# A scan's rows stored, summed and normed one chunk later in the transfers' order

## The chip, the cores and the metric

The kernel runs on one core of a Trainium2 chip. The metric is the device time of one execution in microseconds; the kernel before took a median of 1601.38 us over three runs (1596.47 to 1603.47). The engines are TensorE (PE, with its weight loads PEld), VectorE (DVE), ScalarE (ACT), GpSimd (POOL) and SyncE (SP). SP computes nothing here: it issues most of the transfers, strictly one after the other.

## The reference

The input is one sequence of 1024 tokens with 1024 features. Two layers follow each other, each `h = h + W_out(mixer(rmsnorm(h)) * silu(z))`, and a last RMSNorm. Layer 0 is a chunked spatial gate. Layer 1 is a Mamba-2 mixer, and the change lies in it:

```python
cb = jnp.einsum('bclgn,bcsgn->bclsg', Cm, Bm)
w_ls = (cb[..., None] * decay * dt[:, :, None])
y_diag = jnp.einsum('bclsgj,bcsgjp->bclgjp', w_ls, x)
states = jnp.einsum('bclgn,bclgj,bclgjp->bcgjpn', Bm, decay_to_end * dt, x)
_, prev = lax.scan(step, init, (states, chunk_decay))
y_off = jnp.einsum('bclgn,bcgjpn,bclgj->bclgjp', Cm, prev, jnp.exp(dA_cs))
y = y_diag + y_off + x * d_skip
gated = rmsnorm((y * silu(z)) per group of 256, norm_w)
return gated @ w_out
```

There are 8 groups of 256 inner features (4 heads of 64) and 8 chunks of 128 tokens. Within a group the chunks hang on each other by the carried state. The gated rows of each group are normed over the group's 256 features, token by token, and then multiplied by the output weights.

## The kernel before, in words

Layer 1's scan is one loop over 56 chunks, groups 0 to 6 with 8 chunks each (`scans`, L1705). Group 7 comes after it (`last_steps`, L1677), woven into the first products with the output weights. The scan stands in a region whose order is written by hand: every engine, SP's queue too, issues the region's instructions in the order in which the code names them. What follows the region is ordered by a planner, by estimated times, and may be put between them.

One step of the loop, for chunk `n`, names in this order: the chunk's products on PE (`pe_b`, L1576: `yy` from the decay-weighted matrix and the carried state, L1582 and L1586, and the new state's sum `sp`, L1593); some matmuls of the projection that makes a later group's `x`, `B` and `C` (`project`, tiles `ab`, with weight loads `wr` and splits at L111 and L112); the transposes for chunk n+2 (`pe_a`, `tp`); the state's update and the chunk's output on VectorE (L1612, L1618, L1621); the weights of chunk n+1 (L1573); the decay of chunk n+2 on ScalarE (L1555, L1557); the carried state on GpSimd (L1603); the tokens of chunk n+2 (L1563 to L1568); the gate, which multiplies the output into the `z` rows on GpSimd (L1628); one queued step of the convolution for the projected group (L1281, L1287); and the load of the decay rows of chunk n+3 (`load`, L1544, tile `wl`, four buffers).

Rows come and go by half groups of four chunks. `prefetch` (L1505) loads for a half group `xbc` (only in groups 0, 1, 3 and 5, whose projections were made earlier and spilt), and `ze`: two rows of `z` (L1513) and four broadcast rows of decays (`ecs`, L1517). It is named at chunk 0 for the second half of the same group, and at chunk 4 for the first half of the next. In groups 2, 4, 6 and 7 `x` and `bc` come straight from the projection, which starts a new `x` or `bc` tile at chunk 4 of each group.

A finished half group is treated in the next half. At chunk 4 or 0 its gated rows, which lie in its `ze` tile, are squared on ScalarE (L1633, tile `gsq`) and stored (L1635, to `g_d`). At chunk 5 or 1 GpSimd adds the two rows of squares (L1638). At chunk 7 or 3 PE sums them over the features within `pe_b` (L1645), ScalarE copies the sums to a small tile `srow` (L1649), and SP stores them (`sum_c`, L1652, to `ss_d`). `group_rstd` (L1655) reads the sums of a whole group back as a column (`sv`, L1660) at chunk 4 of the next group; VectorE and GpSimd work out the reciprocal root at chunk 6 (L1666, L141) and chunk 7 (L150 to L153, tile `rvv`), and SP stores it (L1673, to `rs_d`). The output products read `g_d` and `rs_d` later (L1813, L1805).

Tiles of one tag share a fixed number of buffers. A new tile waits until all that used its buffer are done, transfers included:

```python
def s8(shape, name, dt=F32):
    return sb.tile(shape, dt, name=name, tag="s8", bufs=16)
def q4(shape, name):
    return sb.tile(shape, F32, name=name, tag="q4", bufs=6)
```

`s8` buffers (8 KB per partition) hold the split input of the projections (`hh` and `hl` for four quarters, 8 tiles), the table of token values `tk`, and every `x`, `bc`, `xbc` and `ze`. `q4` buffers hold `cw`, the working tile of a chunk, and `gsq`. `k2` holds `wl`; `k1` (three buffers) holds the carried state, a product `t1`, and `srow`.

Of the kernel before, what the change touches and what calls it, by code (L numbers as in the profile page):

```python
# [8 lines left out]
F32 = mybir.dt.float32  # L9
# [6 lines left out]
P = 128  # L16
# [6 lines left out]
G = 8  # L23
# [6 lines left out]
def kernel(  # L30
# [21 lines left out]
    nc = tc.nc  # L52
    x = x[0]
    out = out[0]
# [22 lines left out]
    def tiny(shape, name):  # L77
        return sb.tile(shape, F32, name=name, tag="tiny", bufs=8)
# [65 lines left out]
    def rsqrt_b(dst, v, r, n, rows=P):  # L144

        u = tiny([P, 8], "ru")[:rows, :n]
        if n == 1:
            nc.vector.scalar_tensor_tensor(u, r, v, r, ALU.mult, ALU.mult)
        else:
            nc.vector.tensor_tensor(u, r, r, ALU.mult)  # L150
            nc.vector.tensor_tensor(u, u, v, ALU.mult)
        nc.vector.tensor_scalar(u, u, -0.5, 1.5, ALU.mult, ALU.add)
        nc.vector.tensor_tensor(dst, r, u, ALU.mult)  # L153
# [398 lines left out]
    for gp in range(G // 2):  # L552
# [4 lines left out]
        if gp == 1:  # L557
# [9 lines left out]
            for h in range(2):  # L567
# [9 lines left out]
                for k in range(4):  # L577
                    g = h * 4 + k
# [941 lines left out]
    class Scan:  # L1520
# [110 lines left out]
        def squares(self, th):  # L1631
            sq = self.sq = q4([P, 2, 512], "gsq")
            nc.scalar.activation(sq, self.z(4 * th, 4), AF.Square)  # L1633
            if self.g < G - 1:
                nc.sync.dma_start(out=gd[self.g][:, :, th * 512:(th + 1) * 512], in_=self.z(4 * th, 4))  # L1635

# [3 lines left out]
        def sum_b(self, pr=None):  # L1640
            pr = sm("pr") if pr is None else pr
            n = 1 if self.g < G - 1 else 2
            for m in range(n):
                for h in range(2):
                    nc.tensor.matmul(out=pr[h * 64:h * 64 + 1, 0:256], lhsT=ones[:, 0:1],  # L1645
                                     rhs=self.sq[:, m, h * 256:(h + 1) * 256], start=m == 0, stop=m == n - 1)
            self.sr = sb.tile([P, 256], F32, name="srow", tag="k1", bufs=3)
            for h in range(2):
                nc.scalar.copy(out=self.sr[h * 64:h * 64 + 1], in_=pr[h * 64:h * 64 + 1, 0:256])  # L1649

# [4 lines left out]
    def group_rstd(g, t0, n):  # L1655


        c = n // P
        sv = tiny([P, 8], "sv")[:, 0:c]
        nc.sync.dma_start(out=sv, in_=ss_d[g, t0:t0 + n].rearrange("(p c) -> p c", c=c))  # L1660
        behind = lambda i: nullcontext() if i is None else tc.issue_after(i.ins)
        got = []

        def guess(after=None):
            with behind(after):
                nc.vector.tensor_scalar(sv, sv, 1.0 / 256, NORM_EPS, ALU.mult, ALU.add)  # L1666
                got.append(rsqrt_a(sv, c))

        def tail(after=None, queue=nc.gpsimd):
            rv = tiny([P, 8], "rvv")[:, 0:c]  # L1670
            with behind(after):
                rsqrt_b(rv, sv, got[0], c)
            queue.dma_start(out=rs_d[g, t0:t0 + n].rearrange("(p c) -> p c", c=c), in_=rv)  # L1673

        return guess, tail

    def last_steps():  # L1677

        sc = Scan(G - 1, V)

        def a(c):
            sc.load(c), sc.pe_a(c), sc.decay(c), sc.tokens(c), sc.weights(c)

        a(0)
        yield
        for c in range(8):
            if c < 7:
                a(c + 1)
                yield
            sc.pe_b(c), sc.carry(c), sc.update(c), sc.out(c)  # L1690
            last = sc.gate(c)
            if c == 1:
                prefetch(G - 1, 1)
                rs = group_rstd(G - 2, 0, T)
            if c in (2, 3):
                rs[c - 2](last)
            if c % 4 == 3:
                sc.squares(c // 4), sc.sum_b(), sc.sum_c(c // 4)
            if c == 3:
                half = group_rstd(G - 1, 0, 512)  # L1700
            if c in (4, 5):
                half[c - 4](last)
            yield

    def scans():  # L1705

        chunks = [(g, c) for g in range(G - 1) for c in range(8)]
        N = len(chunks)
        scan, rs, ran = {}, {}, [0]
        total = 32 * len(plain)  # L1710

        def project(upto):
            while ran[0] < upto:
                next(pj, None)
                ran[0] += 1

        def at(f, n, *a):
            if 0 <= n < N:
                g, c = chunks[n]
                if g not in scan:  # L1720
                    scan[g] = Scan(g, nc.gpsimd)
                getattr(scan[g], f)(c, *a)

        prefetch(0, 0)
        project(AHEAD // 2 + 1)
        while todo or late:
            convolve()
        for n in range(2):
            at("load", n)
        drain(1)  # L1730
        for n in range(2):
            at("decay", n)
        drain(len(queue))
        at("pe_a", 0), at("tokens", 0), at("weights", 0)
        drain(len(queue))
        project(AHEAD)
        at("pe_a", 1), at("tokens", 1), at("weights", 1)
        at("load", 2)
        for n, (g, c) in enumerate(chunks):
            want = lambda f: AHEAD + (total - AHEAD) * (n + f) // N  # L1740
            p = g if c >= 4 else g - 1
            at("pe_b", n, scan[p] if c % 4 == 3 and p >= 0 else None)
            project(want(.5))
            at("pe_a", n + 2)
            at("update", n)
            at("out", n)
            if n > 0:
                at("weights", n + 1)
            at("decay", n + 2)
            at("carry", n + 1)  # L1750
            at("tokens", n + 2)
            at("gate", n)
            drain()
            at("load", n + 3)
            th = 0 if c >= 4 else 1
            if p >= 0:
                sc = scan[p]
                if c % 4 == 0:
                    sc.squares(th)
                elif c % 4 == 1:  # L1760
                    sc.sum_a()
                elif c % 4 == 3:
                    sc.sum_c(th)
            if g > 0:
                if c == 4:
                    rs[g] = group_rstd(g - 1, 0, T)
                elif c == 6:
                    rs[g][0]()
                elif c == 7:
                    rs[g][1](None, nc.sync)  # L1770
            if c == 0:
                prefetch(g, 1)
            if c == 4:
                prefetch(g + 1, 0)
            project(want(1))
        project(total)
        sc = scan[G - 2]
        drain(len(queue))
        sc.squares(1), sc.sum_a(), sc.sum_b(), sc.sum_c(1)

    def interleave(a, na, b, nb):

# [80 lines left out]
    def into_end():  # L1863
        rs7 = []

        def hook(n, c):
            if (n, c) == (2, 0):
                bo.fetch(2, 2)
                rs7.extend(group_rstd(G - 1, 512, 512))
                rs7[0]()  # L1870
                bo.fetch(22, 0)
            elif (n, c) == (2, 1):
                bo.fetch(2, 3)
                rs7[1](None, nc.scalar)
                bo.fetch(22, 1)
                bo.sums(2, 0)
            elif (n, c) == (2, 2):
                bo.fetch(22, 2)
                bo.sums(2, 1)
            elif (n, c) == (2, 3):  # L1880
                bo.fetch(22, 3)
                bo.sums(2, 2)
            elif n in (6, 4):
                if (n, c) == (6, 0):
                    bo.sums(2, 3)
                if c % 2:
                    bo.fetch({6: 4, 4: 5}[n], c - 1)
                bo.sums(n, c)
                if (n, c) == (6, 2):
                    weigh_left(0)  # L1890
            elif n == 5:
                bo.prep_last(c)
                if c == 1:
                    weigh_left(1)
                if c == 3:
                    bo.prep_unit(0)

        bo.ran = Out.ORDER
        for n in (2, 6, 4, 5):
            for _ in bo.product(n, hook):  # L1900
                pass
        bo.prep_unit(1)
        r1 = bo.rstd_half(1)
        for tt in range(4):
            bo.last_mm(tt)
            if 0 < tt < 3:
                bo.prep_unit(tt + 1)
            if tt:
                bo.post(3, tt - 1)
                bo.rstd_a(0, tt - 1)  # L1910
            finish_b(1, tt, r1[:, tt:tt + 1])
            if tt:
                finish_b(0, tt - 1, bo.rstd_b(0, tt - 1))
        bo.post(3, 3)
        bo.rstd_a(0, 3)
        finish_b(0, 3, bo.rstd_b(0, 3))
# [33 lines left out]
```

## Time and profile before

| | |
|---|---|
| median of three runs | 1601.38 us (1596.47 to 1603.47) |
| the profiled execution's own time | 1599.88 us |
| its span, first to last instruction | 1598.2 us |
| TensorE busy, share of the span | 1506.0 us, 94% |
| VectorE, ScalarE, GpSimd busy | 1055.3, 777.0, 418.7 us |
| mean granted TensorE clock | 0.973 |
| scan of groups 0 to 6, from the first chunk | 1069 to 1360 us |

Each row of a timeline gives the start in us, the duration in us, the engine, the source line, the operation and the tiles, written ahead of read ones, and in brackets the idle time before it and what ended it. Rows of one line that follow each other are merged with their count. `SPq` is SP's queue: a gap between two of its rows is time in which the next transfer waited for a buffer, for its data, or for an earlier transfer. A wait is put down to what ended last.

### The profile page before, as it was taken

The numbers are of one execution on the slowest core, as the hardware profiler recorded it, in microseconds if no ns is written. First come the engines' busy times: TensorE is split into PE (matmuls) and PEld (weight loads), VectorE is DVE, ScalarE is ACT, GpSimd is POOL, SyncE is SP. The second block draws the span as 40 slices with busy tenths as digits, with TensorE's granted clock in tenths as the row PEclk, the third lists the DMA queues.
The fourth block names the chain that finished last, engine by engine and source line by source line (L and its number), as shares of the span: only waits on it lengthen the run. The fifth ranks groups of instructions, "written<-read, shape, count | busy, mean of one in ns | idle before, by whom it ended". The sixth has DMA issues, their size and how long they took to land.

```text
span 1598.2 us, 21253 instructions
## 1 busy us (share of the span) xinstructions
PE 1506.0 (94%) x7834; PEld 1239.8 (78%) x7834; DVE 1055.3 (66%) x1706; ACT 777.0 (49%) x1247; POOL 418.7 (26%) x443
## 2 busy tenths in 40 slices
PE   5799999999999999998999999989999999979988
PEld 4799988888888887876788787767777777757766
DVE  7966566666666554777637377757777767658656
ACT  4522233323222354555555455646766677544444
POOL 3601010000000131220011312126777765231231
PEclk7999999999999999999999999999999999989999
DMA  5153332332333999755367878776565665795992
GB/s 173 41 191 127 105 109 100 110 111 97 111 108 125 323 261 256 162 139 129 105 154 177 165 165 158 174 208 194 156 176 160 194 172 145 238 249 174 229 237 107
DMA packets 176919, 260.21 MB, mean 163 GB/s; under 512 B 16320, under 2 KB 102960, under 8 KB 173616
## 3 DMA queue, kind: packets, MB, share of 16 engines
q1 hardware_dynamic: 124992, 169.45, 34.3%
q0 software_dynamic: 41888, 71.58, 23.0%
q10 hardware_dynamic: 9936, 17.83, 3.1%
q8 instruction: 62, 1.02, 0.3%
q14 instruction: 41, 0.34, 0.1%
HBM read 185.61 MB, written 51.18 MB: 148 GB/s over the span
## 4 chain that ended last, share of the span: by engine, by line
PE 59%; issue 14%; DMA 9%; DVE 9%; ACT 6%; POOL 1%; ACTq 0%; SPq 0%; POOLq 0%; DVEq 0%
PE acc L136 10%; PE acc L134 9%; PE acc L135 9%; PE ab L134 4%; PE ab L136 4%; PE ab L135 4%; DMA ya<-ya 2%; PE yy L1582 2%; DMA wl<-cs_d 2%; PE yy L1586 2%; PE ao L134 2%; PE ao L135 2%; PE ao L136 2%; PE sp L1593 2%; ACT wh L111 2%
## 5 line engine op out<-in xcount | busy, mean ns | idle before, releaser
L134 PE MATMUL acc<-hh,wh 128*128 128x512 f32 x868 | 343.9, 396 | 15.4 <-ACT u L292 7.6
L136 PE MATMUL acc<-hh,wl 128*128 128x512 f32 x868 | 341.6, 394 | 1.7 <-DVE wl L112 1.6
L135 PE MATMUL acc<-hl,wh 128*128 128x512 f32 x868 | 340.8, 393 | 0.0
L134 PEld LDWEIGHTS acc<-hh,wh 128*128 128x128 f32 x868 | 164.8, 190 | 52.3 <-ACT u L292 9.3
L112 DVE TENSOR_TENSOR wl<-wr,wh 128x1024 fp32r<-128x1024 f32 (+1 forms) x99 | 118.1, 1194 | 128.2 <-ACT wh L111 128.1
L136 PEld LDWEIGHTS acc<-hh,wl 128*128 128x128 f32 x868 | 164.5, 190 | 40.2 <-DVE wl L112 5.6
L135 PEld LDWEIGHTS acc<-hl,wh 128*128 128x128 f32 x868 | 164.8, 190 | 33.4
L111 ACT CAST wh<-wr 128x1024 fp32r<-128x1024 f32 (+1 forms) x113 | 116.4, 1030 | 102.8 <-PE acc L135 57.9
L292 ACT COPY u<-acc 128x512 f32<-128x512 f32 x117 | 67.7, 583 | 197.4 <-PE acc L136 195.7
L136 PE MATMUL acc<-wh,hl 128*128 128x256 f32 x448 | 130.4, 291 | 13.2 <-DVE hl L395 13.2
L134 PE MATMUL acc<-wh,hh 128*128 128x256 f32 x448 | 131.2, 293 | 3.8 <-DVE vt L331 2.5
L135 PE MATMUL acc<-wl,hh 128*128 128x256 f32 x448 | 129.7, 290 | 1.3 <-DVE wl L405 1.3
L134 PE MATMUL ab<-hh,wh 128*128 128x512 f32 x256 | 116.5, 455 | 1.4 <-ACT zt L977 1.4
L1555 ACT ACTIVATE wl<-wl,tk 128x128 f32<-128x128 f32 x256 | 81.9, 391 | 64.1 <-DMA wl<-cs_d 63.8
L135 PE MATMUL ab<-hl,wh 128*128 128x512 f32 x256 | 101.7, 397 | 3.2 <-DVE hl L112 3.2
L136 PE MATMUL ab<-hh,wl 128*128 128x512 f32 x256 | 102.1, 399 | 0.0
L136 PEld LDWEIGHTS acc<-wh,hl 128*128 128x128 f32 x448 | 88.9, 198 | 14.3 <-DVE hl L395 14.3
L134 PEld LDWEIGHTS acc<-wh,hh 128*128 128x128 f32 x448 | 89.1, 199 | 4.8 <-issue 2.9
L134 PE MATMUL bo<-wh,xh 128*128 128x512 f32 x192 | 80.1, 417 | 12.7 <-ACT xh L111 7.4
L135 PEld LDWEIGHTS acc<-wl,hh 128*128 128x128 f32 x448 | 89.0, 199 | 1.7 <-DVE wl L405 1.5
L111 ACT CAST xh<-ya 128x1024 fp32r<-128x1024 f32 x40 | 42.0, 1050 | 90.1 <-PE ao L135 41.7
L112 DVE TENSOR_TENSOR xl<-ya,xh 128x1024 fp32r<-128x1024 f32 x40 | 49.0, 1224 | 55.8 <-ACT xh L111 55.7
(324 smaller groups left out, 3286.4 us busy)
## 6 DMA issues: line engine op xcount, KB each, us to landing
wr<-in_a_w_in_dram SPq DMA_DIRECT2D x48, 512.0 KB, 3.8
wl<-cs_d SPq DMA_DIRECT2D x64, 256.0 KB, 6.2
wr<-in_b_w_in_dram SPq DMA_DIRECT2D x30, 512.0 KB, 6.2
ya<-ya POOLq DMA_DIRECT2D x24, 512.0 KB, 15.5
wb<-in_a_w_out_dram SPq DMA_DIRECT2D x10, 1024.0 KB, 15.1
wb<-in_b_w_out_dram SPq DMA_DIRECT2D x10, 1024.0 KB, 13.7
wr<-in_b_w_in_dram SPq DMA_DIRECT2D x36, 256.0 KB, 6.7
v<-v_d SPq DMA_DIRECT2D x8, 1024.0 KB, 4.7
```

The source lines that it names most:

```text
L111: nc.scalar.copy(out=hi, in_=src)
L112: return (eng or nc.vector).tensor_tensor(out=lo, in0=src, in1=hi.bitcast(F32), op=ALU.subtract)
L134: nc.tensor.matmul(out=o, lhsT=l[0], rhs=r[0], start=start, stop=False, **kw)
L135: nc.tensor.matmul(out=o, lhsT=l[0], rhs=r[1], start=False, stop=False, **kw)
L136: nc.tensor.matmul(out=o, lhsT=l[1], rhs=r[0], start=False, stop=stop, **kw)
L292: nc.scalar.copy(out=self.u[n][:, i], in_=a)
L1555: nc.scalar.activation(wl[:, j, :], wl[:, j, :], AF.Relu, scale=-1.0, bias=tokc(2, c, self.g)[:, j:j + 1])
L1582: nc.tensor.matmul(out=yy[f * 64:(f + 1) * 64, pt * P:(pt + 1) * P], lhsT=w[:, j * 64:(j + 1) * 64], rhs=wl[:, j, :], start=True, stop=True)
L1586: nc.tensor.matmul(out=yy[:, 256 + pt * P:384 + pt * P], lhsT=self.state[c - 1][:, pt * P:(pt + 1) * P], rhs=self.x(3, c), start=True, sto ...
L1593: nc.tensor.matmul(out=sp[:, 0:256], lhsT=w[:, 512:640], rhs=w[:, 256:512], start=True, stop=True)
```

## The change

In the scan four things take other places in the order that the code names:

- the store of a finished half group's gated rows is named at chunk 5 or 1, behind the load of the next chunk's decay rows, and not at chunk 4 or 0 ahead of the prefetch;
- the store of the sums' row is named at chunk 4 or 0, behind the next decay load, and not at chunk 3 or 7;
- the read-back of a group's sums is named at chunk 5 and not at chunk 4;
- the store of the norm's result is a function of its own, `put`, named at chunk 0 of the next group ahead of the prefetch, and not at chunk 7.

The sums' row has no tile of its own any more: it is written into the second half of the tile of squares, which by then has been added into the first. Behind the scan and in the last group the same transfers are named through the new functions at their old places.

```diff
         def squares(self, th):
             sq = self.sq = q4([P, 2, 512], "gsq")
             nc.scalar.activation(sq, self.z(4 * th, 4), AF.Square)
+
+        def store(self, th):
             if self.g < G - 1:
                 nc.sync.dma_start(out=gd[self.g][:, :, th * 512:(th + 1) * 512], in_=self.z(4 * th, 4))
...
-            self.sr = sb.tile([P, 256], F32, name="srow", tag="k1", bufs=3)
+            self.sr = self.sq[:, 1, 0:256]
...
-        def tail(after=None, queue=nc.gpsimd):
-            rv = tiny([P, 8], "rvv")[:, 0:c]
+        def tail(after=None):
+            got.append(tiny([P, 8], "rvv")[:, 0:c])
             with behind(after):
-                rsqrt_b(rv, sv, got[0], c)
-            queue.dma_start(out=rs_d[g, t0:t0 + n].rearrange("(p c) -> p c", c=c), in_=rv)
-
-        return guess, tail
+                rsqrt_b(got[1], sv, got[0], c)
+
+        def put(queue=nc.sync):
+            queue.dma_start(out=rs_d[g, t0:t0 + n].rearrange("(p c) -> p c", c=c), in_=got[1])
+
+        return guess, tail, put
...
             if c in (2, 3):
                 rs[c - 2](last)
+            if c == 3:
+                rs[2](nc.gpsimd)
...
             if c in (4, 5):
                 half[c - 4](last)
+            if c == 5:
+                half[2](nc.gpsimd)
...
                 if c % 4 == 0:
                     sc.squares(th)
                 elif c % 4 == 1:
+                    sc.store(th)
                     sc.sum_a()
-                elif c % 4 == 3:
-                    sc.sum_c(th)
+            if c % 4 == 0 and n >= 8:
+                scan[g - 1].sum_c(1 - th)
             if g > 0:
-                if c == 4:
+                if c == 5:
                     rs[g] = group_rstd(g - 1, 0, T)
                 elif c == 6:
                     rs[g][0]()
                 elif c == 7:
-                    rs[g][1](None, nc.sync)
+                    rs[g][1]()
+            if c == 0 and g > 1:
+                rs[g - 1][2]()
             if c == 0:
                 prefetch(g, 1)
             if c == 4:
                 prefetch(g + 1, 0)
             project(want(1))
         project(total)
         sc = scan[G - 2]
+        sc.sum_c(0), rs[G - 2][2]()
         drain(len(queue))
-        sc.squares(1), sc.sum_a(), sc.sum_b(), sc.sum_c(1)
+        sc.squares(1), sc.store(1), sc.sum_a(), sc.sum_b(), sc.sum_c(1)
...
-                rs7[1](None, nc.scalar)
+                rs7[1](), rs7[2](nc.scalar)
```

## The prediction

> **What bounds the kernel now.** I read the page's head first, then the windows of the scan and of the stretch behind it, then the list of waits and the transfer queue's timeline, and last the other engines' timelines beside it.
>
> ```profile
> span 1598.2 us, 21253 instructions
> ```
>
> Windows (length, busy time by engine, granted clock, DMA share, GB/s): the scan that the change edits, and the stretch of the last group after it.
>
> ```profile
> 1069.00:1360.00 291.00, 284.19 (x1735) 215.94 (x1734) 209.15 (x446) 195.21 (x417) 197.82 (x225) 0.99 0.61 167
> 1400.00:1440.00 40.00, 28.93 (x130) 21.04 (x130) 23.27 (x43) 19.57 (x39) 12.00 (x12) 0.83 1.04 254
> ```
>
> TensorE (PE) is busy for 284.2 of the scan's 291 us: 6.8 us of holes are all that any order of transfers could win there, beside the clock lost behind them. In the second stretch 11.1 us are idle with the DMA engines full.
>
> What does wait in the scan is ScalarE, and it waits for the decay rows that SP loads:
>
> ```profile
> ACT wl L1555 <- DMA wl<-cs_d: 54.9, 13, 8.0
> ```
>
> That happens once per half group, since each half group's store and prefetch stand in SP's queue before the next decay load. SP at group 2, chunk 4 (rows from 1172.34; 1172.34 is the fifth of 14 stores, so group 2's first half) and at group 3, chunk 0 (rows from 1192.96):
>
> ```profile
> 1172.34 0.60 SPq L1635 DMA_DIRECT2D g_d<-ze  x1
> 1173.03 0.55 SPq L1660 DMA_DIRECT2D sv<-ss_d  x1
> 1173.64 0.83 SPq L1510 DMA_DIRECT2D xbc<-xbc_d  x1
> 1180.17 0.58 SPq L1513 DMA_DIRECT2D ze<-z_d  x1
> 1180.81 2.52 SPq L1517 DMA_DIRECT2D ze<-ecs_d  x4
> 1183.42 0.53 SPq L1544 DMA_DIRECT2D wl<-cs_d  x1
> ...
> 1192.96 0.32 SPq L1673 DMA_DIRECT2D rs_d<-rvv  x1
> 1193.37 0.38 SPq L1544 DMA_DIRECT2D wl<-cs_d  x1
> 1193.84 0.59 SPq L1635 DMA_DIRECT2D g_d<-ze  x1
> ...
> 1200.00 1.32 SPq L1544 DMA_DIRECT2D wl<-cs_d  x2
> ```
>
> Two things are to be seen. Between 1174.47 and 1180.17 SP stands still before the load of `ze`: it has no buffer. And at group 3 the load issued at 1200.00 is late, which opens a hole on PE (below).
>
> **The buffer that is missing.** `ze`, `xbc`, `x`, `bc` and the split input share 16 buffers of 8 KB (tag s8). At chunk 4 of group 2 there live: 8 of the split input, 1 of `tk`, `x` and `bc` of group 2, `x` of group 4 and the first part of its `bc`, and both `ze` halves of group 2: 15. `xbc` of group 3 is the 16th, its `ze` would be the 17th. It takes the buffer of the `ze` half whose store was issued at 1172.34, and the last reader of that half beside the store is the squares:
>
> ```profile
> 1179.08 1.06 ACT L1633 ACTIVATE gsq<-ze 128x1024 f32<-128x1024 f32 x1
> ...
> 1187.83 1.28 ACT L1555 ACTIVATE wl<-wl,tk 128x128 f32<-128x128 f32 x4 [4.92 <-DMA wl<-cs_d]
> ```
>
> They end at 1180.14, and the load goes at 1180.17. The same count gives 17 at chunk 4 of group 4 (for group 5), and nowhere else: in spilt groups the first `xbc` half is free by chunk 4 (16 in all), and at chunk 0 the last group's `x`, `bc` or `xbc` are free.
>
> **The change part by part.** No transfer and no compute instruction is added or removed: 14 stores, 16 sums' rows, 9 loads and 9 stores of the norm, as before. Only places move.
>
> (a) *The store goes from chunk 4 (0) to chunk 5 (1), behind the prefetch.* The prefetch of group 3 at chunk 4 now cannot get the buffer of group 2's first half, because what frees it stands behind the prefetch in the same queue. It has to wait for another of the 16. The first to come free is group 2's `bc`, whose last reader is PE's product with the carried state in chunk 7; `x` follows only with VectorE's output of chunk 7 (L1621 below), which in the new order waits too.
>
> ```profile
> 1186.03 0.66 PE L1582 MATMUL yy<-wl,cw 128*64 128x128 f32 x8 [0.58 <-PE ab L136]
> 1186.62 0.71 PE L1586 MATMUL yy<-bc,state 128*128 128x128 f32 x4
> ...
> 1191.34 0.66 PE L1582 MATMUL yy<-wl,cw 128*64 128x128 f32 x8
> ```
>
> That product ends at 1186.62 + 0.71 = 1187.33. So `ze` moves from 1180.17 to 1187.33: 7.16 us. Up to there nothing else stops: chunks 5 to 7 have their decay rows (three chunks ahead), `xbc` is loaded, and chunk 7's weights come on VectorE before the step that waits for `sv`. Queued behind the waiting load on SP are the four `ecs` loads, the decay load of the next chunk 0, the store, `sv`, two weight loads and three further decay loads. ScalarE stands at that chunk's decay, with the sums' copy and the next decay behind it. VectorE:
>
> ```profile
> 1187.57 0.22 DVE L1666 TENSOR_SCALAR sv<-sv 128x8 f32<-128x8 f32 x1
> 1187.71 0.41 DVE L1618 TENSOR_TENSOR t<-yy,ze 128x256 f32<-128x256 f32 x1
> 1188.05 0.59 DVE L1621 SCALAR_TENSOR_TENSOR cw<-x,dsk,yy 128x128 f32<-128x128 f32 x2
> 1189.81 0.98 DVE L1573 TENSOR_TENSOR wl<-wl,cw 128x512 f32<-128x512 f32 x1 [1.17 <-ACT wl L1557]
> ...
> 1192.76 0.17 DVE L153 TENSOR_TENSOR rvv<-rr,ru 128x8 f32<-128x8 f32 x1
> ```
>
> The chain load, decay, weights (end 1189.81 + 0.98 = 1190.79), `yy` has 1191.34 - 1190.79 = 0.55 us to spare, so PE waits 7.16 - 0.55 = **6.6 us** at the first chunk of group 3. VectorE's `sv` step would follow `sv` at about 1187.33 + 3.25 (to the decay load) + 0.53 + 0.60 + 0.1 = 1191.9, plus its landing:
>
> ```profile
> DMA to landing us min/median/max: 2.9/3.0/3.0
> ```
>
> so at 1194.9; its output work of 1.2 us ends at 1196.1, before the decay at 1189.8 + 7.2 = 1197.0. It adds nothing, with 0.9 us to spare.
>
> Group 4 to 5, the same rows of SP, VectorE and PE:
>
> ```profile
> 1265.17 0.58 SPq L1513 DMA_DIRECT2D ze<-z_d  x1
> ```
>
> ```profile
> 1275.56 0.69 DVE L1573 TENSOR_TENSOR wl<-wl,cw 128x512 f32<-128x512 f32 x1 [1.91 <-ACT wl L1557]
> ```
>
> ```profile
> 1271.61 0.71 PE L1586 MATMUL yy<-bc,state 128*128 128x128 f32 x4
> ...
> 1276.35 0.66 PE L1582 MATMUL yy<-wl,cw 128*64 128x128 f32 x8
> ```
>
> 1272.32 - 1265.17 = 7.15, less 1276.35 - 1276.25 = 0.10 of slack: **7.05 us**. Together 13.65.
>
> (b) *The clock behind a hole.* The two holes that the scan has now, at chunk 4 of groups 3 and 5, are followed by a slow clock:
>
> ```profile
> 1213.40 0.66 PE L1582 MATMUL yy<-wl,cw 128*64 128x128 f32 x8 [1.75 <-ACT wl L1557]
> ```
>
> ```profile
> 1298.98 0.44 PE L1582 MATMUL yy<-wl,cw 128*64 128x128 f32 x4 [1.97 <-ACT wl L1557]
> ```
>
> ```profile
> 1214.00:1218.00 4.00, 4.00 (x15) 3.07 (x14) 3.37 (x6) 3.97 (x4) 4.00 (x4) 0.57 0.68 235
> 1299.50:1303.50 4.00, 4.00 (x15) 3.22 (x13) 3.14 (x6) 3.97 (x4) 3.95 (x4) 0.57 0.27 98
> ```
>
> 4 us at 0.57 lose 4 x 0.43 = 1.7 us each. No hole of 7 us in this loop is shown; the clock of 0.83 over 1400 to 1440 loses 6.8 us around 11.1 us of holes. I bound the loss by 1.7 and 3.4 each and take 2.0, nearest to the same loop's rows: **+4.0**.
>
> (c) *What becomes earlier.* Today's two holes come from the load at 1200.00 (and its twin in group 5). In the new order the decay load and the store from 1193.37 to 1193.84 + 0.59, 1.1 us, no longer stand between the norm's result and that load, but the result itself does: `rvv` ends at 1192.93, the store of it goes at 1192.96. It moves with VectorE's weights by 7.2, so the load goes 7.2 - 1.1 = 6.1 us later while PE is 6.6 + 2.0 later. The 2.5 us gained exceed the hole of 1.75 (in group 5: 9.05 - 6.1 = 2.95 against 1.97), so both holes and their slow clock go: -(1.75 + 1.97 + 3.4) = **-7.1**. Lower bound nothing, if landing stays the limit.
>
> (d) *The rest.* At the other chunk 4s the prefetch no longer waits for the store and the decay load goes some 5 us earlier; PE has no hole there, so 0. The sums' row in the squares' tile frees one of three small buffers and holds a `q4` buffer a chunk longer: at most three `cw` and two square tiles live in six, so 0; without that spare, the token step would wait for a row's landing. The norm's guess has `sv` issued at 1173.03 and used at 1187.57, so one chunk of 5 us less is covered by 14.5. In the last two phases the same transfers go in the same places.
>
> Sum: 13.65 + 4.0 - 7.1 = **+10.5** on the profiled execution's 1599.88 us (span 1598.2 and 1.7 around it), 1610.4. It lies 1.5 under the runs' median of 1601.38, so the forecast is **1612**; with the bounds of (b) and (c) it adds 9.9 to 20.5 us to 1601.4, and with 4 us either way for the order behind the scan (below) its own range is 1607 to 1621.
>
> [...]
>
> **Rivals.** *Faster, no wait for a buffer.* If `ze` of groups 3 and 5 finds a buffer (my count one too high), SP runs through, the holes of (c) close and PE wins 7.1 us: 1594. For it: no other prefetch stops in this way. Against: the 5.7 us stop ending with the squares. It decides from one free buffer on.
>
> *No change.* The scan ends 10 us later, but transfers already under way for the last phase go on, and its 11.1 us of holes at full DMA shrink by as much: 1602. Against: those transfers stand in SP's queue behind the scan's, and their buffers are freed by PE.
>
> *Slower by more.* `sv` lands over 0.9 us late, or ScalarE's backlog (it has 195 of 291 us busy) delays chunk 1 as well, and (c) wins nothing: 13.65 + 6.8 = 20.5 and 2 us at each place: 1626.
>
> *The change does something else behind the scan.* The order behind the scan is the planner's, and it follows from estimated times that I don't know; I allow 4 us either way, a third of the 11.1 us of holes there, in the forecast's own range.
>
> **How the numbers follow.** Forecast 0.60, faster 0.10, no change 0.17, more 0.13. About 0.5%, 8 us, is what a measurement can tell. Of the forecast's cases about seven in ten lie over 1609.4. Slower 0.42 + 0.13 = 0.55, same 0.18 + 0.17 = 0.35, faster 0.10. The range 1599 to 1622 leaves out the faster case and most of the slowest.
>
> **What will show it.** SP's load of `ze` at chunk 4 of groups 2 and 4 ends its wait within 0.2 us of the end of L1586 of chunk 7; PE has holes of 6 to 7 us before the `yy` of groups 3 and 5; ScalarE's waits for `wl` fall elsewhere; no hole before chunk 4 of groups 3 and 5. I am wrong if SP passes these prefetches without a stop, or if the holes are there and the end is not later.

## The result, and the profile after

The changed kernel takes a median of 1612.83 us (1608.38 to 1614.55) against 1601.33 us (1596.47 to 1603.47): a ratio of 1.0069, 95% interval 1.0049 to 1.0089. It is slower by some 11 us. The profiled execution took 1612.19 us. Head of its page:

```profile
span 1610.2 us, 21256 instructions
```

SP's queue after the change, at chunk 4 of groups 2 and 4 (start, duration, line, transfer):

```profile
1166.99 0.51 SPq L1654 DMA_DIRECT2D ss_d<-gsq  x1
1167.59 0.34 SPq L1510 DMA_DIRECT2D xbc<-xbc_d  x1
1186.52 0.58 SPq L1513 DMA_DIRECT2D ze<-z_d  x1
1187.16 2.51 SPq L1517 DMA_DIRECT2D ze<-ecs_d  x4
1189.77 0.53 SPq L1544 DMA_DIRECT2D wl<-cs_d  x1
1190.40 0.57 SPq L1637 DMA_DIRECT2D g_d<-ze  x1
1191.02 0.60 SPq L1662 DMA_DIRECT2D sv<-ss_d  x1
...
1278.93 0.58 SPq L1513 DMA_DIRECT2D ze<-z_d  x1
```

SP issues `xbc` and then nothing for 18.6 us, with the decay row, the store and `sv` behind it. TensorE's timeline (in brackets the idle time before a row and what ended it):

```profile
1185.78 0.71 PE L1586 MATMUL yy<-bc,state 128*128 128x128 f32 x4
...
1198.00 1.12 PE L1582 MATMUL yy<-wl,cw 128*64 128x128 f32 x8 [7.42 <-DVE wl L1573]
...
1220.89 0.66 PE L1582 MATMUL yy<-wl,cw 128*64 128x128 f32 x8
...
1278.19 0.71 PE L1586 MATMUL yy<-bc,state 128*128 128x128 f32 x4
...
1290.24 1.12 PE L1582 MATMUL yy<-wl,cw 128*64 128x128 f32 x8 [7.29 <-DVE wl L1573]
...
1313.10 0.66 PE L1582 MATMUL yy<-wl,cw 128*64 128x128 f32 x8
```

The product with the carried state ends at 1185.78 + 0.71 = 1186.49 and at 1278.90; both loads of `ze` go 0.03 us later. Two holes of 7.4 and 7.3 us stand before the first chunk of groups 3 and 5. At chunk 4 of these groups (1220.89 and 1313.10) no hole is left. The windows right behind the new holes (the third number from the end is the granted clock):

```profile
1199.00:1203.00 4.00, 4.00 (x12) 3.09 (x11) 2.78 (x7) 2.51 (x8) 1.75 (x3) 0.50 0.81 148
1291.30:1295.30 4.00, 4.00 (x13) 3.14 (x12) 2.12 (x6) 1.38 (x5) 1.68 (x3) 0.50 0.83 190
```

The starts of `yy` in the two traces give the whole account, each term as the difference of a step's length, after less before:

| step | predicted us | measured us |
|---|---|---|
| chunk 7 to chunk 0 of groups 3 and 5 (the holes) | +6.6, +7.05 | 12.81 - 5.31 = +7.50, 12.64 - 5.32 = +7.32 |
| chunk 0 to 1 (slow clock) | +2.0, +2.0 | 7.23 - 4.53 = +2.70, 7.19 - 4.92 = +2.27 |
| chunk 3 to 5 (holes gone, with their slow clock) | -7.1 together | 10.69 - 14.11 = -3.42, 10.69 - 14.34 = -3.65 |
| chunk 6 to 7 of both groups | 0 | +0.66, +0.67 |
| chunk 5 to 6 of group 6 | 0 | 4.98 - 6.03 = -1.05 |
| scan, sum | +10.5 | +13.0 |
| behind the scan | 0, with 4 either way | -0.15 |

The scan begins 0.87 us earlier in the profile after, so the spans differ by 12.0; the medians differ by 11.5.

### The profile page after: what moved, and what is told of

Read it like the earlier page. It is cut to its first block, busy times and chain, and to the rows that moved or that the text cites. A ratio compares the mean times of both kernels' runs of the same rounds, so it can differ in the third digit from the quotient of the medians.

```text
span 1610.2 us, 21256 instructions
## 1 busy us (share of the span) xinstructions
PE 1506.1 (94%) x7834; PEld 1240.6 (77%) x7834; DVE 1056.4 (66%) x1706; ACT 777.7 (48%) x1247; POOL 418.5 (26%) x443
## 4 chain that ended last, share of the span: by engine, by line
PE 70%; DVE 10%; DMA 9%; ACT 5%; issue 4%; POOL 1%; SPq 1%; ACTq 0%; POOLq 0%; DVEq 0%
PE acc L136 13%; PE acc L134 13%; PE acc L135 13%; PE ab L134 4%; PE ab L136 4%; PE ab L135 3%; DMA ya<-ya 3%; PE yy L1582 2%; PE yy L1586 2%; PE mx L635 2%; PE ao L134 2%; PE sp L1593 2%; PE ao L135 2%; PE ao L136 2%; PE bo L135 2%
## 5 line engine op out<-in xcount | busy, mean ns | idle before, releaser
L134 PE MATMUL acc<-hh,wh 128*128 128x512 f32 x868 | 343.3, 396 | 14.8 <-ACT u L292 7.0
```

What stands on the lines that cost most here:

```text
L134: nc.tensor.matmul(out=o, lhsT=l[0], rhs=r[0], start=start, stop=False, **kw)
```

## The experiments

All ratios are to the kernel before, run on the same chip with them. The kernel before took medians of 1598 to 1600 us there.

| kernel | ratio | 95% interval |
|---|---|---|
| changed, the rows' store first again | 0.9973 | 0.9954 to 0.9992 |
| changed, `ze` asked for late | 0.9959 | 0.9939 to 0.9978 |
| before, rows' store alone moved | 1.0080 | 1.0055 to 1.0105 |
| before, `ze` asked for late | 0.9998 | 0.9983 to 1.0013 |
| changed, one buffer less in demand | 0.9948 | 0.9927 to 0.9969 |
| before, norm's result alone moved | 0.9984 | 0.9967 to 1.0001 |
| before, norm's result moved and `ze` late | 0.9965 | 0.9948 to 0.9981 |
| changed, `sv` first | 1.0075 | 1.0048 to 1.0101 |
| changed, the holes filled | 1.0158 | 1.0123 to 1.0192 |
| changed, `ze` late and the norm's result at chunk 1 | 0.9938 | 0.9915 to 0.9960 |

**Is it the rows' store?** The first experiment undoes that one part of the change and nothing else.

```diff
-                    sc.squares(th)
+                    sc.squares(th), sc.store(th)
                 elif c % 4 == 1:
-                    sc.store(th)
                     sc.sum_a()
```

> The changed kernel with one part undone: the store of a half group's rows stands at chunk 4 or 0 again, ahead of the prefetch; sums, norm and the sums' row stay as changed. Theory (buffer): the load of ze at chunk 4 of groups 2 and 4 goes when the squares end, some 6 us ahead of the changed kernel's 1186.52, and the holes of 7.4 and 7.3 us before the first chunk of groups 3 and 5 fall under 0.7 us; the holes of 1.8 and 2.0 us at chunk 4 of groups 3 and 5 come back, because the loads for these chunks stand behind the same prefetch as in the kernel before: 1600 to 1604 us. Rival (norm's chain: VectorE waits for sv, which is read a chunk later): holes of over 4 us stay before groups 3 and 5: 1608 or more. Rival (the moved norm alone closes the holes at chunk 4): 1594.

TensorE before the first chunk and at chunk 4 of group 3, with the store first:

```profile
1192.51 0.66 PE L1582 MATMUL yy<-wl,cw 128*64 128x128 f32 x8
...
1212.72 0.66 PE L1582 MATMUL yy<-wl,cw 128*64 128x128 f32 x8
```

Both holes are gone, the large ones and those at chunk 4, and the kernel beats the one before (0.9973). The first half of the theory stands; the second half, that the holes at chunk 4 would come back, falls. The last rival was right that they stay closed. Whether the norm's result alone closes them is not told apart here, since the sums stay moved too.

The mirror image puts `sc.store(th)` at chunk 5 or 1 in the kernel before, and nothing else.

> The kernel before with only the store of the gated rows moved to chunk 5 or 1; sums, norm and sums' row as before. Theory (buffer): the same lock, ze of groups 3 and 5 waits for the product with the carried state of chunk 7. Since sv is read here ahead of the prefetch, VectorE does not wait for its landing, so the two holes are about 1 us shorter than in the changed kernel: 6.3 to 6.6 us each, and the time is 1609 to 1611 us. Rival (norm's chain is what costs): no hole over 1 us before groups 3 and 5, 1601 us.

```profile
1197.67 1.12 PE L1582 MATMUL yy<-wl,cw 128*64 128x128 f32 x8 [6.29 <-ACT srow L1651]
...
1289.40 0.91 PE L1582 MATMUL yy<-wl,cw 128*64 128x128 f32 x6 [7.21 <-ACT srow L1651]
```

The store alone makes the whole loss: 1.0080, with holes of 6.29 and 7.21 us (ScalarE's copy of the sums, which stands behind the late decay, ends last). The second is 0.6 longer than expected: there the decay row took 5.25 us from its issue at 1281.39 to ScalarE's start at 1286.64, against 4.29 us in the first (1190.62 to 1194.91).

**Is it the buffer?** One kernel keeps the changed order and needs one buffer less.

```diff
-        if g in xbc_d:
+        if (g, th) in ((3, 0), (5, 0)):
+            st["xbc", th] = H2["A11"][0].bitcast(F32)
+        elif g in xbc_d:
```

> The changed kernel, its whole order kept, with one buffer less in demand: the first xbc half of groups 3 and 5 is not loaded, the scan reads a tile of the projections' split input in its place (so two loads of 1 MB and the right values of two half groups are left out). Theory (a 17th buffer is missing, and that alone makes the lock): ze is the 16th and SP passes at chunk 4 of groups 2 and 4 without a stop; no hole over 0.7 us before groups 3 and 5 nor at their chunk 4; the time is that of the kernel with ze asked for late: ratio to the kernel before 0.994 to 0.997. Rival (ze waits for the store or the squares of the rows for another reason, say the lanes of the queue): the stop stays, ratio 1.007.

SP's queue at chunk 4 of group 2 of this kernel:

```profile
1165.32 0.52 SPq L1656 DMA_DIRECT2D ss_d<-gsq  x1
1165.93 0.58 SPq L1515 DMA_DIRECT2D ze<-z_d  x1
1166.56 2.51 SPq L1519 DMA_DIRECT2D ze<-ecs_d  x4
1169.19 0.52 SPq L1546 DMA_DIRECT2D wl<-cs_d  x1
```

The stop of 18.6 us is gone with one buffer, in an order that is otherwise that of the change. TensorE's waits over the scan name 3.0 us before `yy`, none longer than 0.6, and the ratio is 0.9948. Part of that could be the two loads of 1 MB that are left out (the scan computes with other rows in these two half groups); the next kernel leaves nothing out.

It asks for the `ze` half of groups 3 and 5 at chunk 6, when the stored half is free:

```diff
...
             if c == 4:
-                prefetch(g + 1, 0)
+                prefetch(g + 1, 0, (0,) if g in (2, 4) else (0, 1))
+            if c == 6 and g in (2, 4):
+                prefetch(g + 1, 0, (1,))
```

> The changed kernel, but the ze half for group 3 (5) is asked for at chunk 6 of group 2 (4) and not at chunk 4, so that the stored half is free by then; everything else as changed. Theory (buffer): SP passes without a stop, no hole over 0.7 us before groups 3 and 5 nor at their chunk 4, sv on time: 7.1 us under the kernel before, 1594 us (1591 to 1597). Rival (norm's chain): holes before groups 3 and 5 stay, 1608 or more. Rival (only the lock goes, the holes at chunk 4 come back since PE is early again): 1601.

SP's load of `ze` and TensorE's first chunk and chunk 4 of group 3:

```profile
1177.30 0.59 SPq L1515 DMA_DIRECT2D ze<-z_d  x1
```

```profile
1188.45 0.66 PE L1584 MATMUL yy<-wl,cw 128*64 128x128 f32 x8
...
1208.67 0.66 PE L1584 MATMUL yy<-wl,cw 128*64 128x128 f32 x8
```

0.9959, which is 1595 us on the scale of 1601.33; the scan is 7.2 us shorter than before, with no hole over 0.6 us. The buffer theory holds.

**What closes the holes at chunk 4?** The same edit in the kernel before:

> The kernel before, all its stores and norm steps in place, but the ze half for groups 3 and 5 is asked for at chunk 6 and not at chunk 4. Theory (the holes at chunk 4 come from the order around the norm's result at chunk 0): the result comes 1.2 and 1.9 us earlier, because VectorE no longer waits for the decay in front of it, so the holes of 1.75 and 1.97 us shrink to 0.6 and 0.1 and their slow clock goes: 1595 to 1598 us. Rival (the holes come from the prefetch's own traffic at chunk 0): they stay, 1601 us.

No gain (0.9998), and my forecast falls. The holes are still 1.76 and 1.43 us, though SP no longer stops at chunk 4 of groups 2 and 4, so that stop is not what opens them. Part of the missing gain went elsewhere: the hole before chunk 6 of group 6 grew from 0.97 to 2.01 us, with a granted clock of 0.57 over the 4 us from 1354.80, and the two steps around it took 2.65 us more. For the holes at chunk 4, the order at chunks 7 and 0 remains, or the prefetch's own traffic (the rival). There, in the kernel before, the sums' row (issued at 1190.59) and the norm's result (1192.96) wait at the head of SP's queue, and the decay row of chunk 3 goes behind them at 1193.37, only 1.2 us ahead of the prefetch. With the store first:

```profile
1186.73 1.48 SPq L1544 DMA_DIRECT2D wl<-cs_d  x3
1193.92 0.58 SPq L1637 DMA_DIRECT2D g_d<-ze  x1
1194.59 0.51 SPq L1654 DMA_DIRECT2D ss_d<-gsq  x1
1195.20 0.76 SPq L1677 DMA_DIRECT2D rs_d<-rvv  x1
...
1199.81 3.24 SPq L1544 DMA_DIRECT2D wl<-cs_d  x3
```

The decay row of chunk 3 is the third of those issued from 1186.73 to 1188.21, well ahead of the prefetch, and both waits stand behind it. ScalarE's decay of chunk 4, first of the kernel before and then of the kernel with the store first:

```profile
1208.61 1.28 ACT L1555 ACTIVATE wl<-wl,tk 128x128 f32<-128x128 f32 x4 [8.04 <-DMA wl<-cs_d]
```

```profile
1206.62 1.28 ACT L1555 ACTIVATE wl<-wl,tk 128x128 f32<-128x128 f32 x4 [4.90 <-DMA wl<-cs_d]
```

Counted from the group's first `yy` the decay row of chunk 4 is issued 1200.00 - 1191.34 = 8.66 us before the change and 1199.81 - 1192.51 = 7.30 us here, and it is there 8.6 and 6.8 us after its issue. It goes 1.4 us earlier and lands 1.8 us faster. Why it lands faster is not shown; the other decay row, now well ahead of the burst, is one candidate.

Is the norm's result enough? Its store alone is moved in the kernel before, and then together with the late `ze`:

```diff
...
-                    rs[g][1](None, nc.sync)
+                    rs[g][1](None, None)
+            if c == 0 and g > 1:
+                rs[g - 1][2]()
```

> The kernel before with only the store of the norm's result moved: named at chunk 0 behind the decay load of chunk 3 and the store of the rows, not at chunk 7 ahead of them; rows' store, sums and sums' row as before. Theory (SP stands at chunk 7 for the norm's result, with the decay load of chunk 3 behind it, which then lands among the prefetch): the load goes some 2 us earlier than 1193.37, the holes at chunk 4 of groups 3 and 5 (1.75 and 1.97 us) fall under 0.7 us and the slow clock behind them goes: ratio to the kernel before 0.996 to 0.998, about 1595 to 1598 us where the kernel before takes 1601. Rival (the sums' row, which stands there too and waits for ScalarE, holds the load as well): holes of over 1 us stay, ratio 0.999 to 1.001.

> The kernel before with two edits: the norm's result stored as in the run above, and the ze halves for groups 3 and 5 asked for at chunk 6; the rows' store stays at chunk 4 and 0. Theory (the rows' store has no share in the gain): as the changed kernel with ze asked for late, ratio 0.995 to 0.997, no hole over 0.7 us at groups 3 and 5. Rival (the rows' store or the sums must move too): ratio 0.999 to 1.001, holes of over 1 us at chunk 4 of groups 3 and 5 stay.

TensorE at chunk 4 of groups 3 and 5 with the norm's result alone moved, and its waits for `yy` with both edits:

```profile
1212.04 0.66 PE L1582 MATMUL yy<-wl,cw 128*64 128x128 f32 x8 [0.86 <-ACT wl L1557]
...
1296.75 0.66 PE L1582 MATMUL yy<-wl,cw 128*64 128x128 f32 x8 [1.67 <-ACT wl L1557]
```

```profile
PE yy L1584 <- PE ab L136: 2.9, 5, 0.6
PE yy L1584 <- DVE wl L1575: 1.2, 1, 1.2
```

Alone it is between the two expectations: 0.9984, an interval that touches 1, and holes of 0.86 and 1.67 us. The sums' row, still at chunk 7, waits until 1189.59 in that trace, and the decay row of chunk 3 follows at 1190.20, 0.6 us after the first `yy` of group 3 at 1189.61; before the change it was 1193.37 - 1191.34 = 2.0 us after it, and with the store first some 4 us ahead of it. The decay row of chunk 4 is issued 1196.84 - 1189.61 = 7.23 us after the first `yy`, as early as with the store first, yet lands 10.4 us later, at 1207.25, though the decay row of chunk 3 goes 2.4 us ahead of the prefetch. So the earlier issue alone does not close the holes, and that row's place alone does not make the landing fast. Together with the late `ze` the holes at chunk 4 close and the ratio is 0.9965. Its interval does not separate it from 0.9959, but does from the 0.9998 of the late `ze` alone, from which it differs by the norm's result only. So neither the rows' store nor the sums had to move to close these holes. The wait of 1.2 us stands before chunk 6 of group 6; it goes only where the rows' store moves, as (d) below shows.

**Two sizes.** The prediction let `sv` pass with 0.9 us to spare. VectorE and ScalarE of the changed kernel show that it did not pass:

```profile
1196.28 0.17 DVE L1668 TENSOR_SCALAR sv<-sv 128x8 f32<-128x8 f32 x1 [9.47 <-DMA sv<-ss_d]
...
1197.21 0.69 DVE L1573 TENSOR_TENSOR wl<-wl,cw 128x512 f32<-128x512 f32 x1
```

```profile
1195.53 0.63 ACT L1557 ACTIVATE wl<-wl 128x512 f32<-128x512 f32 x1
```

`sv` is there 1196.28 - 1191.02 = 5.3 us after the start of its issue (5.2 by the trace's own count of issue to landing, which gave the 3.0 that were taken), and VectorE's weights start at 1197.21 though the decay ended at 1196.16. So `sv` was put ahead of the prefetch again (`c == 4` in place of `c == 5` for `group_rstd`):

> The changed kernel with the read-back of the sums (sv) at chunk 4 again, ahead of the prefetch that waits; everything else as changed. Theory (the lock, lengthened by VectorE's wait for sv): the wait of ze does not move, VectorE no longer stands for sv, and the holes before groups 3 and 5 shrink from 7.4 and 7.3 us by 0.9 to 1.0 us each: 2 us less than the changed kernel, ratio to the kernel before 1.005 to 1.007. Rival (sv costs nothing): the holes stay at 7.3 to 7.4.

```profile
1198.48 1.12 PE L1582 MATMUL yy<-wl,cw 128*64 128x128 f32 x8 [7.23 <-DVE wl L1573]
```

```profile
1195.72 1.28 ACT L1555 ACTIVATE wl<-wl,tk 128x128 f32<-128x128 f32 x4 [12.93 <-DMA wl<-cs_d]
```

The rival holds: VectorE no longer waits for `sv`, but the holes stay, at 7.23 and 7.56 us. The decay row itself now came later: 5.3 us from its issue at 1190.43 to 1195.72, against 1194.22 - 1189.77 = 4.45 in the changed kernel. With the store alone moved the row took 4.29 us and the hole was 6.29: 1.0 us more of landing, 0.9 us more of hole. In all four holes of these two kernels the hole is 1.9 to 2.0 us longer than the row's landing (4.29 and 6.29, 5.25 and 7.21, 5.29 and 7.23, 5.64 and 7.56). In the changed kernel it is 3.0 and 3.1 us longer (4.45 and 7.42, 4.20 and 7.29): there VectorE's wait for `sv` adds to it. So either of the two landings can set the hole, and here taking one away left the other, which had grown. Why the row lands later is not shown.

For the slow clock, TensorE was to be kept busy through the holes:

```diff
             yy = sm("yy")
+            if c == 0 and self.g in (3, 5):
+                for _ in range(26):
+                    nc.tensor.matmul(out=yy[:, 256:464], lhsT=ident, rhs=par[:, 0:208], start=True, stop=True)
```

> The changed kernel with 26 extra fp32 products of 208 columns (ident by a table of constants, into columns of yy that no one reads) on TensorE ahead of the first chunk's yy in groups 3 and 5, so that the array is busy in the two holes; nothing else. They take about 0.28 us each by the 128-column products of the state (0.16 us from one to the next), 7.2 us in all. Theory (a hole costs its length and then 2.3 to 2.7 us of slow clock): chunk 0 to chunk 1 of groups 3 and 5 takes 4.5 to 5.0 us and not 7.2, the clock behind is 0.9 or more, and the time falls by 4 to 5 us against the changed kernel: ratio to the kernel before 1.003 to 1.005. Rival (the chunks behind the hole are slow for another cause, as the transfers that pile up): they stay at 7.2 us, ratio 1.007.

```profile
1194.18 11.22 PE L1582 MATMUL yy<-par,ident 128*128 128x208 f32 x52 [5.89 <-ACT cw L1567]
1205.34 0.66 PE L1585 MATMUL yy<-wl,cw 128*64 128x128 f32 x8
...
1209.86 0.66 PE L1585 MATMUL yy<-wl,cw 128*64 128x128 f32 x8
```

```profile
1194.30:1204.30 10.00, 10.00 (x47) 9.91 (x48) 3.79 (x10) 4.42 (x13) 3.60 (x4) 0.82 0.90 234
1205.40:1209.40 4.00, 4.00 (x27) 3.31 (x27) 2.29 (x6) 0.10 (x1) 0.92 (x2) 1.00 0.83 209
```

As a filling this failed. The extra products waited 5.89 us themselves, for the accumulator that ScalarE's copy behind the late decay sets free, and took 11.2 us instead of 7.2, so the time rose to 1.0158. For the clock it still tells something: the chunk that follows takes 4.52 us and not 7.23, at a clock of 1.00; the slow clock was spent on the extra products (0.82 over their first 10 us). It does not exclude that the transfers, by then further on, had a part.

**A version that beats both.** To the changed kernel with `ze` late, one more step: the norm's result is stored at chunk 1 (`c == 1` in place of `c == 0` for `rs[g - 1][2]()`).

> The changed kernel with ze asked for late (as in the earlier run) and the norm's result stored a chunk later still, at chunk 1 behind the prefetch. SP no longer stands some 3 us ahead of the prefetch at chunk 0. Theory: no hole of TensorE is left there that this could close, so nothing: ratio 0.994 to 0.998, as with ze asked for late alone (0.9959). Rival (the earlier prefetch meets other transfers and makes a decay row late): holes over 1 us, ratio 0.998 or more.

0.9938 (0.9915 to 0.9960), 1591 us on the scale of 1601.33, just past the fast edge of what was expected; its interval includes the 0.9959, so the last step's own worth is not shown. It is faster than the kernel before and the changed one by more than their intervals. TensorE's waits from 1065 to 1372 us, the scan and 26 us behind it:

```profile
PE yy L1584 <- PE ab L136: 3.0, 5, 0.6
PE pr L1649 <- POOL gsq L1642: 0.7, 1, 0.7
```

## Why the prediction was right

**The lock (a)** came as worked out: the 17th buffer, `ze` released 0.03 us behind the product with the state, and both holes where they were named. Its size was 14.8 us instead of 13.65. The step that failed is that `sv` lands 3.0 us after its issue and the decay row behind `ze` as soon as before; `sv` took 5.2, and where it was out of the way the decay row took 5.3 in place of 4.4.

**The slow clock (b)** was 4.97 us, not 4.0: in windows of 0.5 us it was 0.50 for 5.8 and 5.7 us from the end of the long holes (to 1203.8 and 1295.9), against 3.4 us behind each of the short ones of the kernel before (1214.6 to 1218.0 and 1299.9 to 1303.3). The bounds of 1.7 and 3.4 held.

**The holes at chunk 4 (c)** brought 7.07 of the 7.1 us forecast, but the reason given was only partly right, so a match this close is luck. I let the order give 1.1 us and TensorE's lateness the rest. With the lateness taken away (store first, `ze` late, one buffer less) the holes are closed all the same: the changed order is enough without it. With the store alone moved, where TensorE is late and the norm's result and the sums keep their places, they are closed too. What the 1.1 us left out is the landing: I moved the issue of the decay rows and kept the time they take to arrive, and that fell by 1.8 us with the store first. And 1.33 us of the gain came back: the wait of 0.6 us before chunk 7, which groups 1, 2 and 4 have before and after the change, was missing in groups 3 and 5 behind the slow clock, and stands there too now (+0.66 and +0.67).

**The rest (d)** was nearly 0 in sum, but one step of it failed: I wrote that TensorE has no hole at the other chunk 4s, so that an earlier decay load wins nothing. There was one behind chunk 4 of group 6, before chunk 6. First the kernel before, then the changed one:

```profile
1352.04 0.66 PE L1582 MATMUL yy<-wl,cw 128*64 128x128 f32 x8 [0.97 <-DVE wl L1573]
```

```profile
1364.20 0.66 PE L1582 MATMUL yy<-wl,cw 128*64 128x128 f32 x8
```

Its going is the -1.05 of the table. With the store alone moved it goes as well (4.98 us for the step of 6.03), and it stands with 0.93 to 2.01 us in all five kernels that store the rows at chunk 4 or 0 and in none of the seven that store them at chunk 5 or 1.

**The time.** That 1612 was forecast and 1612.83 measured is closer than the sum deserves: the scan's terms were 2.5 us short (10.5 against 13.0), and 1.0 us of that came back outside the scan and 0.5 us between the profiled executions and the medians.

**The rivals.** *Faster, no wait for a buffer* has the right price: with a free buffer the changed order takes 0.9948 (some 1593 us, with two loads left out), and 1594 us was forecast. The count of buffers was right, so it did not occur. *No change* is refuted: TensorE waits before the `bo` products as long as before the change (7.3 and 7.4 us for ScalarE's `xh`), and the stretch behind the scan gave 0.15 us back. *Slower by more* had its first step, `sv` over 0.9 us late, but the holes at chunk 4 closed.

## What to carry to other kernels

In a queue that issues strictly in order, as SP's did here with everything behind a stop of 18.6 us, a load must not stand ahead of the transfer that frees its buffer: count the buffers that live at the moment of each load, and when the count is one too high, look for the next buffer that comes free, since its release is the new start of everything queued behind (here `ze` went 0.03 us after it). Storing later is only free if the next load asks later too; here the late store alone took the ratio to 1.0080, some 13 us, and the whole change with the load two chunks later won 6 to 7. A store that waits for a result is best named behind the loads that the next steps need, because a load's issue and its landing can both move, here by 1.4 and 1.8 us.

## What the runs showed of the hardware

Holes of almost the same length had a slow clock behind them or none. In the kernel before, 1.75 and 1.97 us were followed by 0.57 over 4 us (shown with the prediction). In the kernel before with `ze` late, the hole and the windows behind it and behind its twin of 1.43 us:

```profile
1216.00 0.66 PE L1584 MATMUL yy<-wl,cw 128*64 128x128 f32 x8 [1.76 <-ACT wl L1559]
```

```profile
1216.60:1220.60 4.00, 4.00 (x23) 3.22 (x22) 3.79 (x6) 3.97 (x4) 4.00 (x4) 1.00 0.69 249
1301.00:1305.00 4.00, 4.00 (x24) 3.16 (x22) 3.79 (x6) 3.97 (x4) 3.96 (x4) 1.00 0.27 98
```

The hole of 1.67 us with the norm's result alone moved likewise kept a clock of 1.00 over the 4 us behind it, while the hole of 2.01 us in group 6 of the kernel before with `ze` late had 0.57 behind it. So between 1.67 and 1.97 us the length alone does not decide. The four holes of 7.2 to 7.6 us in the changed kernel and in the one with `sv` first made the next chunk 2.70, 2.27, 1.76 and 1.60 us longer than in the kernel before. Why short holes of the same length end differently was not measured, so this stays open.
